# Operands of the second token group written straight into the hop tiles, operand pairs stored together, and the first steps of the layer put in another order

## The chip, the cores and the metric

One core of one Trainium2 chip runs the whole kernel. The metric is device time in microseconds of one launch, the median of several runs. TensorE (PE) multiplies, VectorE (DVE) and ScalarE (ACT) work on tiles, GpSimd (POOL) casts and copies now and then, and SyncE (SP) issues nearly all DMAs. Each engine takes its instructions in the order in which they stand in its own row; semaphores hold it until its inputs are there.

## The reference

One layer with 2048 tokens and 256 context tokens of width 1024; both head groups read one input projection, and one output projection joins them.

```python
shift, scale, gate = split(silu(c) @ w_ada + b_ada, 3)          # ada; also for c_ctx
h  = rmsnorm(x, norm_w)   * (1 + scale)   + shift               # (2048, 1024)
hc = rmsnorm(ctx, norm_w) * (1 + scale_c) + shift_c             # (256, 1024)
p  = h  @ w_in                                                  # 5*1024 + 4*1024 columns
pc = hc @ w_in[:, :5*1024]
q, v, f_f, f_b ... = hgrn_prep(p)                               # 8 heads of 128
o_f, o_b = chunk_scan(forward), chunk_scan(backward)            # states begin from the context's
y_hg = rmsnorm(o_f + o_b, onorm_w) * silu(p[gate columns])
y_cv = bg * conv3(cg * h_conv, conv_w) * silu(gate_conv)
out  = rmsnorm(x + gate * (concat(y_hg, y_cv) @ w_out), final_norm_w)
```

## The kernel before

**Products.** The 2048 tokens are four groups of 512 (`GW`), x0 to x3. A product of a group with a pair of weight column blocks is made in seven products over half the tokens instead of eight (`seven`), in fp16 with a high and a low part: three matmuls per step, L890, L891, L892. The weights give seven operands (A11, S1, ...), and each group gives seven: B11, T1, T2, B21, T3, B22, T4 (`OPS`). One operand of a group is 128 x 2 (high, low) x 4 (`HK`) x 256 (`HW`) in fp16, 512 KB. Group x0 is special in its first use, where its plain high and low parts (four tiles `plain`) are multiplied without the seven (`plain` units).

**Windows.** The work is a list of windows; a window is one head (or one block of the convolution) on one group. Windows 0 to 3 are head 0 on groups 0 to 3; windows 4 to 7 head 1, and so on. In each, the products of a few units (q, v, f, the gate) run on PE, while the chunk scan of the head (Q, K, A, S on DVE, ACT and PE) runs between them. The context's products (`ctx` units, with the operands `hc`) run in the windows of head 0.

**Operands of a group.** For groups 1 to 3 `norm_group` makes the operands: it loads four row tiles of 128 tokens (`load`, tiles xt), sums their squares on ACT (`square`, L238), scales them by the reciprocal root (`norm`, L244 on ACT and L246 on DVE, in turn), and then makes four turns. A turn (`turn`, `combine`, L321 on) transposes two feature blocks on PE (L253, eight transposes), applies scale and shift on ACT (L274), makes sums on DVE (L328, L329, L331, L337), casts high parts on ACT or POOL (L279, L281) and subtracts to get low parts on DVE (L298), into `pair` tiles, and stores each operand's share in DRAM (`Hd`, L300): seven stores in a turn. When all four turns of a group are stored, `prefetch` loads the seven operands into tiles of `hp` (L1306, `hop`), one DMA of 128 rows of 4 KB each, as far as the nine (`HOPS`) hop tiles allow; `freed` and `taken` count them, and `set_ready` lets a group's loads begin. Every later window that uses the group loads the seven operands again. For x0, whose plain parts are in SBUF, B11, B21 and B22 are stored by `store_first` and the T operands come from four `late` turns (`late_turn`) that read the raw values back from DRAM (`Xd`).

**Order.** What one engine does in which order is set in the program: the products of a window call `tick`, and steps (`paced`, with weights in `PACE`) are issued between them, spread by `merge_steps` over the window. In before, window 0 holds the context's norm and turns, x1's norm and four turns, and x2's loads, norm and first turn; window 1 holds x2's other turns and x3's loads, norm and first turn; window 2 x3's other three; window 3 x0's four late turns. A step is issued behind a given instruction with `tc.issue_after` (`behind` does it for weights, behind the last product that is kept).

**Start.** `modulate` multiplies the conditioning with w_ada as its tiles arrive (1 MB per block of 128 features) and transposes x0's raw blocks (`raw`) between; `modulate_end` takes the result out of PSUM (`ada_r`, L209), transposes it (`ada_t`, L212); `affine` turns it into scale and shift (`ab`).

Of the kernel before, what the change touches and what calls it, by code (L numbers as in the profile page):

```python
# [60 lines left out]
def hybrid_layer(ctx: ExitStack, tc, x, cx, w_ada, b_ada, w_in, w_out, fnorm_w, small_d, masks, ident_d, sel_d, out):  # L61
# [19 lines left out]
    Hd = [{o: dp.tile([P, 2, HK, HW], F16, name=f"Hd{g}{o}", tag=f"Hd{g}{o}") for o in OPS} for g in range(NG)]  # L81
# [125 lines left out]
    def modulate_end(pada):  # L207
        ada_r = ring("ada_r")
        V.tensor_copy(ada_r, pada)  # L209
        ptr = pa_t("ada_t")  # L210
        for q in range(4):
            PE.transpose(ptr[:, q * P:(q + 1) * P], ada_r[:, q * P:(q + 1) * P], ident)  # L212
        V.tensor_tensor(ada, ptr.rearrange("p (q j m) -> p j q m", q=4, j=4)[:, :, :, 0:2],
                        sub(bada, 0, [[4, 4], [1, 4], [0, 2]]), ALU.add)

# [10 lines left out]
    def norm_group(ntile, src, row0, m, nm, first_ops=None, space=q_tile):  # L226
        n = ntile * P
        xs = []
        ssq = sp.tile([P, 16], F32, tag="ssq", name=f"ssq_{nm}", bufs=4)

# [6 lines left out]
        def square(i):  # L237
            S.activation(junk, xs[i], AF.Square, accum_out=ssq[:, i:i + 1])  # L238

        def norm():  # L240
            rstd = rsqrt(ssq[:, :ntile], ntile, 1.0 / D, nm)
# [8 lines left out]
        def transposed(k):  # L250
            pt = pa_t(f"xT_{nm}{k}")
# [72 lines left out]
        def combine(k, a, b, whole):  # L324
# [10 lines left out]
            else:  # L335
# [8 lines left out]
                [paced(0.0, lambda k=k: raw(k)) for k in range(KT)])  # L344
# [12 lines left out]
    def behind(fn):  # L357

        if not last_keep:
            return fn()  # L360
        with tc.issue_after(last_keep[-1].ins):
            fn()
# [661 lines left out]
    def wo_at(name, hl, k):  # L1024
        return wo_home(name, hl)[:, k // HK, k % HK, :]
# [287 lines left out]
    extra_a21 = [[a21_[:, hl, :, i * P:(i + 1) * P] for hl in range(2)] for i in range(2)]  # L1313
    taken[0] = len(plain) + 1 + NCH
# [11 lines left out]
    pada = modulate(lambda k: first[4][k][1](), lambda: next_w(0))  # L1326
# [3 lines left out]
    modulate_end(pada)  # L1330
# [3 lines left out]
    affine(1, 7)  # L1334
    x_norm = [None, x1_norm] + [norm_group(NCH, x, g * GW, 0, f"x{g}") for g in range(2, NG)]

    def store_first():
        for o in ("B11", "B21", "B22"):
            r, half = int(o[1]) - 1, int(o[2]) - 1
            for i in range(HK // 2):  # L1340
                for hl in range(2):
                    SY.dma_start(Hd[0][o][:, hl, 2 * i:2 * i + 2],
                                 plain[r * HK // 2 + i][:, hl, :, half * HW:(half + 1) * HW])

    def set_ready(g):
        ready[0] = max(ready[0], g)
        if g == 1:
# [19 lines left out]
    def run(wi, units, steps):  # L1367
# [20 lines left out]
        for un, (wk, kind, i, fn) in enumerate(units):  # L1388
# [22 lines left out]
            elif kind == "plain":  # L1411
                ps = bank(turn_bank[0], f"u{ui}")
                turn_bank[0] = 1 - turn_bank[0]
                for half in range(2):
                    hs = slice(half * HW, (half + 1) * HW)
                    for k in range(KT):
                        op, kk = w.ops[f"A{i}{k // HK + 1}"], k % HK
                        r = [plain[k // 2][:, hl, k % 2, hs] for hl in range(2)]
# [6 lines left out]
            elif kind == "pair":  # L1425
# [5 lines left out]
                seven(w.ops.get, lambda o, hl, k, i=i: C[i][o][:, hl, k, :], HK, GW, f"{ui}", pair_step,  # L1431
# [167 lines left out]
```

## Time and profile before

| | |
|---|---|
| median of 3 runs | 2181.78 us (2180.26 to 2185.07) |
| profiled execution | 2187.49 us, span 2185.7 |
| granted TensorE clock, mean | 0.990 |
| PE busy | 2089.4 us |
| DVE busy | 1652.1 us |
| ACT busy | 1169.2 us |
| start of the plain products | 44.69 us |
| first product on x1's, x2's, x3's operands | 97.06, 155.77, 197.09 us |

The times of the rows below are counted from the start of the span of the profiled execution. In the timeline a row is a run of equal instructions on one engine: start, time to the end of the last of them, engine, line, operation, output and inputs; in brackets the time that the engine stood idle before it and who released it. An engine that stands idle does no harm unless it is the one that sets the end.

### The profile page before, as it was taken

What the parts mean: (1) busy time and instruction counts of PE and PEld (TensorE: products, weight loads), DVE (VectorE), ACT (ScalarE), POOL (GpSimd) and SP (SyncE); (2) the same over time, 40 slices, a digit from 0 to 9 for tenths busy, and PEclk for the clock granted to TensorE, in tenths of its full rate; (3) what the DMA queues carried; (4) which work ended last, traced back from release to release, by engine and by line L of the source; (5) the groups of instructions that cost most, each with busy time, mean ns of one, the idle gap of its engine ahead of it and who ended that gap; (6) DMA issues with size and microseconds to landing.
All of it is one profiled execution on the core that took longest, in us unless ns stands there. A gap on an engine that the chain in (4) does not pass through costs nothing.

```text
span 2185.7 us, 51899 instructions
## 1 busy us (share of the span) xinstructions
PE 2089.4 (96%) x21563; PEld 1468.2 (67%) x21563; DVE 1652.1 (76%) x3456; ACT 1169.2 (53%) x2341; POOL 157.9 (7%) x239
## 2 busy tenths in 40 slices
PE   5789999999999999999999999999999999999998
PEld 2677688888887988888889887444444444444443
DVE  7887777878779778788687786677787656687775
ACT  7865556666557565666675654344444423333332
POOL 0211111010010110101111000000000000000000
PEclk9999999999999999999999999999999999999999
DMA  9766533433243333333633448923443205633321
GB/s 349 238 205 208 181 132 103 141 116 105 86 159 107 114 114 125 111 108 128 194 123 123 140 156 260 274 97 121 135 139 98 66 30 181 213 124 108 127 85 58
DMA packets 196464, 310.41 MB, mean 142 GB/s; under 512 B 13570, under 2 KB 126594, under 8 KB 194436
## 3 DMA queue, kind: packets, MB, share of 16 engines
q1 hardware_dynamic: 194068, 303.16, 42.5%
q8 instruction: 169, 2.77, 0.5%
q10 hardware_dynamic: 2160, 3.93, 0.5%
q14 instruction: 67, 0.55, 0.1%
HBM read 241.77 MB, written 65.27 MB: 140 GB/s over the span
## 4 chain that ended last, share of the span: by engine, by line
PE 66%; DVE 18%; ACT 8%; DMA 5%; issue 2%; POOL 1%; SPq 0%; POOLq 0%; ACTq 0%; DVEq 0%
PE sa L890 8%; PE sa L891 8%; PE sa L892 8%; PE sb L890 4%; PE sb L891 4%; PE sb L892 4%; PE sa_o L890 2%; PE sa_o L891 2%; PE sa_o L892 2%; DVE e_p L152 2%; PE A L599 2%; PE sc L890 2%; PE sc L892 2%; PE sc L891 2%; DVE K L453 2%
## 5 line engine op out<-in xcount | busy, mean ns | idle before, releaser
L453 DVE TENSOR_TENSOR K<-K,tot 128x512 f32<-128x512 f32 x192 | 133.6, 696 | 60.1 <-PE A L627 27.6
L891 PEld LDWEIGHTS <-e_p 128*128 128x128 f16 x1368 | 134.1, 98 | 60.4 <-issue 10.9
L890 PEld LDWEIGHTS <-e_p 128*128 128x128 f16 x1368 | 134.1, 98 | 59.9 <-DMA hop1T<-Hd1T 2.6
L892 PEld LDWEIGHTS <-e_p 128*128 128x128 f16 x1368 | 134.2, 98 | 52.8 <-issue 1.8
L460 DVE TENSOR_TENSOR Q<-Q,tot 128x512 f32<-128x512 f32 x192 | 132.4, 690 | 44.3 <-PE A L599 30.9
L569 ACT ACTIVATE km<-K 128x512 f32<-128x512 f32 x160 | 109.0, 686 | 69.5 <-DVE K L453 60.0
L890 PEld LDWEIGHTS <-whib_p 128*128 128x128 f16 x912 | 89.3, 98 | 41.2 <-issue 5.0
L890 PEld LDWEIGHTS <-whia_p 128*128 128x128 f16 x912 | 89.4, 98 | 38.5 <-DMA hop3B<-Hd3B 2.8
L891 PEld LDWEIGHTS <-whib_p 128*128 128x128 f16 x912 | 89.4, 98 | 38.2 <-issue 4.1
L891 PEld LDWEIGHTS <-whia_p 128*128 128x128 f16 x912 | 89.3, 98 | 37.7 <-issue 5.6
L892 PEld LDWEIGHTS <-wlob_p 128*128 128x128 f16 x912 | 89.4, 98 | 34.7 <-issue 0.5
L892 PEld LDWEIGHTS <-wloa_p 128*128 128x128 f16 x912 | 89.4, 98 | 34.4
L151 ACT ACTIVATE e_p<-ws_p,sc_p 128x512 f16<-128x512 f32 x108 | 77.2, 717 | 53.4 <-DVE ws_p L413 33.3
L576 POOL COPY qm<-Q 128x512 f32<-128x512 f32 x64 | 55.7, 870 | 630.2 <-DVE Q L460 627.2
L635 POOL COPY A<-Ac 32x128 f32<-32x128 f32 x128 | 68.3, 534 | 371.2 <-ACT A L631 367.2
L897 ACT ACTIVATE u<-sa,sx_w 128x256 f32<-128x256 f32 (+1 forms) x114 | 59.8, 525 | 59.2 <-PE sa L892 48.7
L897 ACT ACTIVATE p<-sb,sx_w 128x256 f32<-128x256 f32 (+1 forms) x114 | 59.4, 521 | 52.9 <-PE sb L892 52.3
L897 ACT ACTIVATE p<-sa,sx_w 128x256 f32<-128x256 f32 (+1 forms) x114 | 59.1, 518 | 47.4 <-PE sa L892 46.6
L152 DVE SCALAR_TENSOR_TENSOR e_p<-ws_p,sc_p,e_p 128x512 f16<-128x512 f32 x108 | 78.5, 742 | 1.0 <-ACT e_p L151 1.0
L813 ACT ACTIVATE cv<-c,small 128x512 f32<-128x512 f32 (+1 forms) x36 | 24.2, 674 | 97.6 <-DVE c L831 52.9
L378 ACT ACTIVATE junk<-ws_p 128x1024 f16<-128x1024 f32 x72 | 75.7, 1051 | 0.2
L151 ACT ACTIVATE hiS_o<-y_o,sc_y 128x1024 f16<-128x1024 f32 x32 | 36.8, 1149 | 72.6 <-PE sa_o L891 32.2
(865 smaller groups left out, 6972.1 us busy)
## 6 DMA issues: line engine op xcount, KB each, us to landing
ws_p<-in_w_in SPq DMA_DIRECT2D x72, 512.0 KB, 4.4
y_o<-yT SPq DMA_DIRECT2D x32, 512.0 KB, 4.2
xt_x<-in_x SPq DMA_DIRECT2D x16, 512.0 KB, 4.6
wa<-in_w_ada SPq DMA_DIRECT2D x16, 512.0 KB, 10.2
Gd<-zs SPq DMA_DIRECT2D x32, 256.0 KB, 3.2
wos<-in_w_out SPq DMA_DIRECT2D x32, 256.0 KB, 3.9
sg<-Gd SPq DMA_DIRECT2D x32, 256.0 KB, 3.8
yT<-y SPq DMA_DIRECT2D x32, 256.0 KB, 2.2
```

What stands on the lines that cost most here:

```text
L151: S.activation(hi, src, AF.Copy, scale=st[:, 0:1])
L152: V.scalar_tensor_tensor(lo, src, st[:, 0:1], hi, ALU.mult, ALU.subtract)
L378: S.activation(junk.rearrange("p (k n) -> p k n", k=KT), stage[i], AF.Abs, accum_out=r)
L453: V.tensor_tensor(m, m, sub(cur, nb + 1, [[2, np_], [-(nb + 1), 2], [0, B]]), ALU.mult)
L460: V.tensor_tensor(m, m, sub(cur, 1, [[2, np_], [nb - 1, 2], [0, B]]), ALU.mult)
L569: S.activation(sub(s.km, 0, [[2 * B, n // (2 * B)], [B, 2], [1, B]]), mix(s.K, n, B, n // (2 * B)), AF.Copy)
L576: G.tensor_copy(sub(qm, 0, [[2 * B, n // (2 * B)], [B, 2], [1, B]]), mix(s.qf, n, B, n // (2 * B)))
L635: G.tensor_copy(A3[js, :, js], s.Ac[js])
L890: PE.matmul(ps, hi[:, k], rh, start=start and k == 0, stop=False, skip_group_check=not start)
L891: PE.matmul(ps, hi[:, k], right(name, 1, k), start=False, stop=False, skip_group_check=not start)
L892: PE.matmul(ps, lo[:, k], rh, start=False, stop=k == nk - 1, skip_group_check=not start)
L897: last_keep.append(S.activation(r, ps, AF.Copy, scale=sx))
```

## The change

Seven things change together.

1. The layout of an operand in SBUF is [128, 4, 2, 256] (block, part, token) rather than [128, 2, 4, 256]. In DRAM the operands lie in rows that belong to a pair: B11 and T3, T1 and T2, B21 and B22 side by side (`Hr`), T4 alone. A turn stores a pair with one DMA, four stores in a turn; a load of one operand of a pair collects 1024 pieces of 512 bytes.
2. In the start, the last two raw transposes of x0 are issued behind the transposes of ada, `ada_r` is copied half by DVE and half by ACT, the context's `affine` is issued behind x0's third low part, and the squares and scales of a group are issued behind the casts and lows of the group before (`follow`).
3. x1's operands are written straight into the tiles that window 1 reads (`own1`: four hop tiles and three Q tiles), with casts of 256 columns; they are stored to DRAM in window 1 (`store_own`, seven DMAs). x1's row tiles lie in weight staging tiles.
4. x2's loads, norm and first turn move from window 0 to window 1, x3's norm stays late in window 1's list and its first turn moves to window 2. x2's row tiles lie in hop tiles, x3's in Q tiles that `own1` frees.
5. x0's four late turns move from window 3 to windows 4 and 5, two each.
6. The weights of the gate are loaded in window 0 still, behind x1's last transposes.
7. The counts in `freed` and `taken` are adapted.

The diff's core:

```diff
+    ROWS = (("B11", "T3"), ("T1", "T2"), ("B21", "B22"), ("T4",))
+    Hr = [{r: dp.tile([P, HK, 2, len(r), HW], F16, name=f"Hd{g}{r[0]}", tag=f"Hd{g}{r[0]}") for r in ROWS}
+          for g in range(NG)]
+    Hd = [{o: Hr[g][r][:, :, :, i] for r in ROWS for i, o in enumerate(r)} for g in range(NG)]
...
-        V.tensor_copy(ada_r, pada)
+        V.tensor_copy(ada_r[:, :HW], pada[:, :HW])
+        S.activation(ada_r[:, HW:], pada[:, HW:], AF.Copy)
...
         def square(i):
-            S.activation(junk, xs[i], AF.Square, accum_out=ssq[:, i:i + 1])
+            follow(casts.get(before), lambda: S.activation(junk, xs[i], AF.Square, accum_out=ssq[:, i:i + 1]))
 
         def norm():
+            follow(lows.get(before), scaled)
...
+            if direct:
+                for i, op in enumerate(ops):
+                    cast(eng, direct[op][:, k, 0], row[:, i * HW:(i + 1) * HW])
+                    low.append(V.tensor_tensor(direct[op][:, k, 1], row[:, i * HW:(i + 1) * HW], direct[op][:, k, 0],
+                                               ALU.subtract))
+                return
...
-            V.tensor_tensor(lo, row, hi, ALU.subtract)
-            for i, op in enumerate(ops):
-                SY.dma_start(Hd[row0 // GW][op][:, :, k], pair[:, :, i])
+            low.append(V.tensor_tensor(lo, row, hi, ALU.subtract))
+            g = row0 // GW
+            if n2 == 2:
+                SY.dma_start(Hr[g][ops][:, k], pair)
+            else:
+                SY.dma_start(Hd[g][ops[0]][:, k], pair[:, :, 0])
...
-    x1_norm = norm_group(NCH, x, GW, 0, "x1", None, wa_hop)
+    own1 = {}
+    x1_norm = norm_group(NCH, x, GW, 0, "x1", None, stage_tile, own1)
...
+    turned = modulate_end(pada)
+    for k in (KT - 2, KT - 1):
+        follow(turned, first[4][k])
...
+    for n_, o in enumerate(OPS):
+        own1[o] = hop_tile(f"hop1{o}") if n_ < 4 else qp.tile([P, HK, 2, HW], F16, tag="Q", name=f"hop1{o}", bufs=6)
+    hop[1] = own1
...
-            early = (ctx_norm[1] + ctx_norm[2] + n1[1] + n1[2] if wi == 0 else n1[2][1:]) + ready_
+            early = (ctx_norm[1] + ctx_norm[2] + n1[1] if wi == 0 else []) + n1[2] + ready_
             if wi == 0:
                 more_params()
-                for _, st in n2[0]:
+                early.insert(0, paced(0.1, store_first))
+                early += [paced(0.1, lambda: next_w(1, 6))]
+            if wi == 1:
+                store_own()
+                for _, st in n1[0]:
                     st()
-                early += [paced(0.1, store_first)]
...
-                early += n2[1] + n2[2][:1]
+                taken[0] += NCH
+                early = n1[1] + [paced(14.0, lambda: None)] + early
+            if n2 is not None and wi:
+                early += [paced("pause", lambda: None)] + n2[0] + n2[1]
             extra = early + extra
-        elif wi == NG - 1:
-            extra = first[3] + extra
+        elif wi in (NG, NG + 1):
+            extra = first[3][(wi - NG) * 2:(wi - NG) * 2 + 2] + extra
```

On PE, at the end of window 0 before: x2's first transposes (xT, two feature blocks x20 and x24 and one of the next turn) stand between the context's last product (u) and window 1's first product (sa on hop1B11).

```order
L1407 MATMUL u6_1123<-hc_128,wloa_p8_277 128x256
L253 MATMUL xT_x20_1082<-ident_132,xt_x20_488 128x128
L253 MATMUL xT_x24_1089<-ident_132,xt_x20_488 128x128
...
L253 MATMUL xT_x24_1089<-ident_132,xt_x23_494 128x128
L253 MATMUL xT_x21_1181<-ident_132,xt_x21_490 128x128
L890 LDWEIGHTS whia_p24_219
L890 MATMUL sa_7_1164<-hop1B11_1013,whia_p24_219 128x256
```

The same place now:

```order
L1444 LDWEIGHTS wloa_p8_265
L1444 MATMUL u6_1008<-hc_116,wloa_p8_265 128x256
L917 LDWEIGHTS whia_p24_207
L917 MATMUL sa_7_1060<-hop1B11_474,whia_p24_207 128x256
L918 LDWEIGHTS whia_p24_207
L918 MATMUL sa_7_1060<-hop1B11_474,whia_p24_207 128x256
```

No transposes stand there any more; x2's first are now 824 rows into PE's list, in window 1. On SP, before, the loads of x1's operands (hop1) stand among the stores of x1's and x2's turns (Hd1, Hd2; 256 pieces):

```order
L1306 DMA hop1B11_1013<-Hd1B11_94 128x2048
L300 DMA Hd1T4_100<-hpT4_x13_979 256x1x256
L1306 DMA hop1T1_1015<-Hd1T1_95 128x2048
L1306 DMA hop1T2_1017<-Hd1T2_96 128x2048
L1306 DMA hop1B21_1019<-Hd1B21_97 128x2048
L300 DMA Hd2T1_102<-hpT1_x20_1099 256x1x256
L300 DMA Hd2T2_103<-hpT1_x20_1099 256x1x256
```

There are no hop1 loads for window 1 now. At the next such place, the loads of x2's operands (hop2) ahead of window 2, SP has now, with x3's row tiles (xt_x30 to xt_x33) among them:

```order
L252 DMA xt_x30_1810<-in_x 128x1024
L252 DMA xt_x31_1812<-in_x 128x1024
L328 DMA Hd2T1_96<-hpT1_x23_1665 128x1024
L328 DMA Hd2B11_95<-hpB11_x23_1670 128x1024
L328 DMA Hd2B21_97<-hpB21_x23_1674 128x1024
L330 DMA Hd2T4_98<-hpT4_x23_1679 128x512
L252 DMA xt_x32_1814<-in_x 128x1024
L1333 DMA hop2B11_1787<-Hd2B11_95 128x8x256
L1333 DMA hop2T1_1789<-Hd2T1_96 128x8x256
...
L1333 DMA hop2T4_1799<-Hd2T4_98 128x2048
L252 DMA xt_x33_1816<-in_x 128x1024
```

A turn's stores are four rather than seven, a load of a pair's operand is 128 x 8 pieces of 256 elements, and x3's fourth row tile is loaded behind all hop2 loads. On PE, window 2's products run from row 1203 to 1743 of the list; x3's first transposes now stand there, among the products on hop2 and the scan's matrices (A0):

```order
L917 MATMUL sc_11_2286<-hop2B21_1793,whia_p8_264 128x256
L274 MATMUL xT_x30_1914<-ident_120,xt_x30_1810 128x128
L274 MATMUL xT_x34_1921<-ident_120,xt_x30_1810 128x128
L626 MATMUL A0_0_1_1967<-q_0_1_1283,ks_0_1_1686 32x32 x9
L274 MATMUL xT_x30_1914<-ident_120,xt_x31_1812 128x128
```

They are rows 1450 on; the last transposes of x3 end at row 1554. Before, x3's first turn stood in window 1 (row 1163) and its last in window 2 (rows 1576 to 1583).

## Rows read from the trace of the kernel before

**Rows 1.** The page: busy us (share of span) and instructions by engine.

```profile
PE 2089.4 (96%) x21563; PEld 1468.2 (67%) x21563; DVE 1652.1 (76%) x3456; ACT 1169.2 (53%) x2341; POOL 157.9 (7%) x239
```

**Rows 2.** Windows: stretch, us, busy by engine, granted clock, DMA share, GB/s.

```profile
50.00:100.00 50.00, 39.58 (x322) 34.02 (x321) 41.45 (x114) 42.80 (x76) 11.25 (x17) 0.88 0.77 244
100.00:150.00 50.00, 42.14 (x562) 34.45 (x560) 44.85 (x111) 33.82 (x62) 8.56 (x13) 0.91 0.72 239
150.00:200.00 50.00, 45.57 (x584) 40.58 (x582) 38.52 (x80) 26.76 (x51) 10.14 (x15) 0.99 0.48 150
200.00:250.00 50.00, 43.94 (x543) 30.49 (x542) 41.28 (x90) 29.16 (x55) 7.58 (x10) 1.00 0.78 252
250.00:300.00 50.00, 49.89 (x709) 43.70 (x708) 35.89 (x89) 27.46 (x66) 3.87 (x6) 1.00 0.38 122
```

**Rows 3.** Windows of 10 us, columns as in group 2.

```profile
90.00:100.00 10.00, 5.35 (x26) 4.56 (x27) 7.65 (x19) 6.48 (x11) 1.58 (x2) 0.52 0.81 272
40.00:50.00 10.00, 5.04 (x24) 3.07 (x25) 8.98 (x29) 7.82 (x15) 3.64 (x4) 0.58 0.93 349
...
230.00:240.00 10.00, 9.02 (x71) 6.80 (x71) 10.00 (x18) 6.27 (x13) 2.69 (x4) 1.00 0.82 250
```

**Rows 4.** Timeline of PE at the starts of units and windows.

```profile
44.69 0.37 PE L1419 MATMUL u<-hop,whia_p 128*128 128x256 f16 x1 [2.59 <-ACT hop L281]
...
94.35 2.42 PE L253 MATMUL xT_x<-ident,xt_x 128*128 128x128 f32 x10 [7.07 <-DVE xt_x L246]
...
97.06 0.37 PE L890 MATMUL sa<-hop1B,whia_p 128*128 128x256 f16 x1 [0.30 <-DMA hop1B<-Hd1B]
...
108.72 0.28 PE L890 MATMUL sa<-hop1T,e_p 128*128 128x256 f16 x1 [2.48 <-DMA hop1T<-Hd1T]
...
155.77 0.27 PE L890 MATMUL sa<-hop2B,whia_p 128*128 128x256 f16 x1
...
197.09 0.28 PE L890 MATMUL sa<-hop3B,whia_p 128*128 128x256 f16 x1 [2.49 <-DMA hop3B<-Hd3B]
...
220.43 0.18 PE L139 MATMUL ss_p<-rb_p 128*128 128x1 bf16 x1 [2.48 <-DVE rb_p L382]
```

**Rows 5.** Timeline around the conditioning's transposes.

```profile
39.35 0.68 DVE L209 COPY ada_r<-pada 128x512 f32<-128x512 f32 x1
...
40.17 0.30 PE L212 MATMUL ada_t<-ident,ada_r 128*128 128x128 f32 x1 [1.47 <-ACT junk L238]
```

**Rows 6.** DVE groups, 69 to 94 us: busy us, mean ns, idle before.

```profile
L298 DVE TENSOR_TENSOR hpB_x<-h_x,hpB_x 128x512 f16<-128x512 f32 x8 | 5.4, 687 | 1.4 <-POOL hpB_x L279 1.3
...
L298 DVE TENSOR_TENSOR hpT_x<-h_x,hpT_x 128x256 f16<-128x256 f32 x4 | 1.7, 419 | 0.5 <-POOL hpT_x L279 0.5
```

**Rows 7.** Timeline: scales of x1 and x2, last lows of x2 and x3.

```profile
65.34 1.18 ACT L244 ACTIVATE xt_x<-xt_x,rsy_x 128x1024 f32<-128x1024 f32 x1
...
93.54 1.42 DVE L246 TENSOR_SCALAR xt_x<-xt_x,rsy_x 128x1024 f32<-128x1024 f32 x2
...
132.66 0.43 DVE L298 TENSOR_TENSOR hpT_x<-h_x,hpT_x 128x256 f16<-128x256 f32 x1 [0.30 <-POOL hpT_x L279]
...
190.49 0.42 DVE L298 TENSOR_TENSOR hpT_x<-h_x,hpT_x 128x256 f16<-128x256 f32 x1 [0.19 <-POOL hpT_x L279]
```

**Rows 8.** Timeline of SP: issues of loads of operands.

```profile
192.47 0.56 SPq L1306 DMA_DIRECT2D hop3B<-Hd3B  x1
...
453.55 0.32 SPq L1306 DMA_DIRECT2D hop10T<-Hd2T  x1
...
1332.14 1.69 SPq L951 DMA_DIRECT2D C0B<-Hd0B  x1
```

**Rows 9.** Windows: two stretches full of loads, columns as in group 2.

```profile
10.00:30.00 20.00, 12.90 (x64) 4.43 (x66) 16.22 (x40) 13.77 (x22) 0.00 (x0) 1.00 1.03 410
1330.00:1340.00 10.00, 10.00 (x94) 9.00 (x92) 6.40 (x14) 2.74 (x6) 0.00 (x0) 1.00 1.18 299
```

**Rows 10.** Tile hop10B on PE: durations ns min/median/max, first and last start.

```profile
L890 PE MATMUL sa<-hop10B,whia_p x8: 272/273/273, 468.2 to 481.9; 128*128 128x256 f16 x8
```

More of the change, by code (lines that the diff above doesn't have):

```diff
@@ L224, in affine, with follow, norm_group @@
         V.tensor_scalar(ab[:, m], ab[:, m], hsc[m][:, 0:1], None, ALU.mult)
-    def norm_group(ntile, src, row0, m, nm, first_ops=None, space=q_tile):
+    def follow(marks, fn):
+        if not marks:
+            return fn()
+        with tc.issue_after(marks[-1].ins):
+            fn()
+    lows, casts = {}, {}
+    def norm_group(ntile, src, row0, m, nm, first_ops=None, space=q_tile, direct=None):
         n = ntile * P
@@ L229, in norm_group @@
         ssq = sp.tile([P, 16], F32, tag="ssq", name=f"ssq_{nm}", bufs=4)
+        before = None if first_ops is not None else "x0" if m else f"x{row0 // GW - 1}"
+        low, high = lows.setdefault(nm, []), casts.setdefault(nm, [])
         def load(i):
@@ L254, in transposed, with raw @@
             return pt
-        def raw(k):
-            pt = transposed(k)
+        def raw(k, space=pa_t):
+            pt = transposed(k, space)
             raws[k] = ring(f"h32_{nm}{k}")
-            if k % 2:
+            if k % 2 and space is pa_t:
                 V.tensor_copy(raws[k], pt)
@@ L343, in norm_group @@
                 [paced("late", lambda k=k: late_turn(k)) for k in range(HK)],
-                [paced(0.0, lambda k=k: raw(k)) for k in range(KT)])
+                [lambda k=k: raw(k, pa_t if k < KT - 2 else px_t) for k in range(KT)])
     class W:
@@ L357, in behind @@
     def behind(fn):
[L359 to L362, printed above, removed]
+        follow(last_keep, fn)
     def load_pair(col0, col1, nm, own=False, a21_at=None):
@@ L1298, in hybrid_layer @@
     for wi, g in enumerate(group_of):
-        if g is not None and wi and g != group_of[wi - 1]:
+        if g is not None and wi > 1 and g != group_of[wi - 1]:
             queue += [(wi, g, o) for o in OPS]
@@ L1324, in hybrid_layer @@
     next_w(0)
-    pada = modulate(lambda k: first[4][k][1](), lambda: next_w(0))
+    pada = modulate(lambda k: first[4][k]() if k < KT - 2 else None, lambda: next_w(0))
     ctx_norm = norm_group(2, cx, 0, 1, "c")
@@ L1333, in hybrid_layer, with store_own @@
         st()
-    affine(1, 7)
-    x_norm = [None, x1_norm] + [norm_group(NCH, x, g * GW, 0, f"x{g}") for g in range(2, NG)]
+    follow(lows["x0"][:3], lambda: affine(1, 7))
+    x_norm = [None, x1_norm] + [norm_group(NCH, x, g * GW, 0, f"x{g}", None, wa_hop if g == 2 else q_tile)
+                                for g in range(2, NG)]
+    for n_, o in enumerate(OPS):
+        own1[o] = hop_tile(f"hop1{o}") if n_ < 4 else qp.tile([P, HK, 2, HW], F16, tag="Q", name=f"hop1{o}", bufs=6)
+    hop[1] = own1
+    def store_own():
+        for o in OPS:
+            SY.dma_start(Hd[1][o], own1[o])
     def store_first():
@@ L1340, in store_first @@
             for i in range(HK // 2):
-                for hl in range(2):
-                    SY.dma_start(Hd[0][o][:, hl, 2 * i:2 * i + 2],
-                                 plain[r * HK // 2 + i][:, hl, :, half * HW:(half + 1) * HW])
+                SY.dma_start(Hd[0][o][:, 2 * i:2 * i + 2],
+                             plain[r * HK // 2 + i][:, :, :, half * HW:(half + 1) * HW])
     def set_ready(g):
         ready[0] = max(ready[0], g)
-        if g == 1:
+        if g == 2:
             freed[0] += NCH
@@ L1417, in run @@
                         op, kk = w.ops[f"A{i}{k // HK + 1}"], k % HK
-                        r = [plain[k // 2][:, hl, k % 2, hs] for hl in range(2)]
+                        r = [plain[k // 2][:, k % 2, hl, hs] for hl in range(2)]
                         PE.matmul(ps[:, hs], op[0][:, kk], r[0], start=k == 0, stop=False)
@@ L1445, in run @@
             pace[1] += 1
-        if wi == 0 and units[-1][1] == "ctx" and len(units) > 2:
+        if wi == 0:
             freed[0] += 5
```

41 lines of the change are left out of this document (18 added, 23 removed).

## The prediction

> **What bounds the kernel now.** I read the page first, then the windows view, then PE's timeline, then SP's. PE is busy for 2089.4 us, 96% of the span [rows 1]; the matmuls are the same before and after, so the time can only move by what PE waits for, or by its clock. The windows view says where it waits: between 50 and 250 us PE is busy 39.58, 42.14, 45.57 and 43.94 of 50 us, and from 250 on 49.89 [rows 2]. So what the change can win or lose at its beginning is won or lost before 250, and a microsecond there is one at the end, since PE is full behind it. The idle time of those four slices is 200 - 171.2 = 28.8 us. The second loss is the clock: 0.58 in 40 to 50 and 0.52 in 90 to 100 [rows 3], each time behind a wait; for those two stretches TensorE ran mostly at 1.2 GHz.
>
> The timeline shows the waits one by one [rows 4]: 2.59 us before the plain products (44.69), 7.07 before x2's first transposes (94.35), 0.30 before the first product of window 1 (97.06), 2.48 for a load of x1's operands (108.72), 2.49 for x3's operands (197.09, the start of window 3), and 2.48 (220.43). Window 2 starts at 155.77. The second column to look at is DVE: 41.45, 44.85, 38.52 and 41.28 of 50 us in the same slices [rows 2]. DVE has 34 us of slack against PE's 29. It is the engine that prepares the operands of groups 1 to 3 (turns and their casts), and the change removes no turn. That is why I don't believe that all of PE's waits can go.
>
> **The head.** The last two raw transposes go behind those of ada, and ada_r is copied half by DVE and half by ACT. Now DVE's copy of the whole tile starts only at 39.35, behind a raw copy of the same size (0.69), takes 0.68, and PE waits 1.47 us until 40.17 [rows 5]. With the raw copy out of the way and two halves side by side on two engines, ada_r is there 0.69 + 0.68/2 = 1.0 us sooner from these rows alone, and up to 1.7 with the square's place on ACT, which the row at 40.17 names as what ended the wait [rows 5]. The context's squares now stand behind x0's casts, which takes some 0.6 us more from the ACT work ahead of the first cast. I put the plain products at 42.4, so -2.3 us (bounds -0.5 and -3.0, the latter a little over the whole 2.59 wait).
>
> **Window 0.** x1's operands are written directly into the hop tiles; no store, no load. x2's norm and first turn leave window 0: PE's 7.07 us wait at 94.35 goes, with the half clock that follows, and so do the 0.30 and the 2.48 of the loads. What then ends last is DVE on x1. One turn is three 128x512 lows at 0.69 us and, on 128x256, one low and four sums of about 0.42 [rows 6], 4.2 us busy, some 4.4 with what lies between; four turns 17.6. With the larger lows cut in 256-wide pieces a turn has 11 operations of 0.42 (they overlap by some 0.08), about 3.8 us, four 15; with the first head's Q and K steps (about 3.5) 18.5. x1's last scale ends at 65.34 + 1.18 = 66.5 on ACT [rows 7], transposes and h_x take two or three more, so the last low stands at 86 to 88 if DVE has nothing else. The first product needs only the first tile's last low and starts at about 85.5: 11.6 us ahead of 97.06 (bounds 84.5 and 88).
>
> **Window 1.** It took 58.7 us (97.06 to 155.77). It now also holds x2's norm and first turn, DVE 1.42 for two scales [rows 7] plus the chain of small operations of the norm (an estimate: a dozen at 0.16 to 0.3, 2.4) and a turn of 4.4, that is 8 us on DVE, beside the 44.85 of 50 it had [rows 2]. So the window is DVE's: x2's last low lies at 131 to 135, about where it was (132.66 + 0.42 [rows 7]), though PE is 11 us ahead. The wait that the change removes in front of window 1 returns inside it, in part. Behind the last low come the stores of one turn and the seven loads. These loads are the other half of the change: a pair is stored with one DMA, but a load then collects pieces of 512 bytes. An old load issues in 0.32 us [rows 8]. The nearest rows for small pieces are the C loads of the convolution, 1.69 us each back to back [rows 8], with 299 GB/s against 410 in the load stretch at 10 to 30 us [rows 9]. The price of a load between those ends is 1.75 us (512 KB at 299 GB/s) against 1.28; a product takes 1.31. While PE eats them as they land, each of six loads costs 0.44 us, 2.6 us a set. That is the upper bound; with a lead it is nothing. Window 2 starts at 140.3 by that (134 + 4.6 for a load, as in front of window 3 [rows 4, 8], + 1.7 for the feed), -15.5 us; bounds 138.5 and 143.
>
> The Trainium skill, page "DMA: Bandwidth & Descriptors", section "Specifications", gives 512 B as the least transfer for line rate. By it these loads would cost what the old ones did, and the 2.6 us here and the 3.5 below would be nothing: rival (d). The 299 against 410 GB/s [rows 9] does not agree with it, so I go by the rows.
>
> **Window 2.** It took 41.3 us. Before, x3's norm and first turn were done in window 1, and its other three turns here; now all four turns are here. Two of x3's four row tiles are loaded before x2's last stores, the third before and the fourth behind the seven hop2 loads on SP, all waiting for Q tiles that x1's operands hold until window 1's last products (T3, B22 and T4). What is queued behind a waiting SP there is the hop2 loads themselves. The transposes of x3 stand 46% down PE's row of window 2 (row 1450 between 1203 and 1743): 19 us in. From there DVE has four turns (4.4 each, 17.8) and the head's Q and K levels (some 8 us of this stretch): 26 us. x3's last low is therefore at 140.3 + 18.5 + 26, about 185, where it was 190.9 (190.49 + 0.42 [rows 7]). The first load was issued at 192.47 [rows 8] and the product stood at 197.09 [rows 4], 4.6 us after. With 512-byte pieces 6 rather than 4.6: window 3 starts at about 191, -6 us; PE, which has 41 us of work there, waits some 8 to 10 us at the end of window 2 instead. So of the 15.5 us gained, 9.5 are given back here. Bounds: -20, if DVE does the turns as they come and PE never waits, and +1, if they start 6 us later and the load is slow.
>
> **Window 3 and after.** The four late turns of x0 (four DVE-heavy steps, DVE 10.00 of 10 us in 230 to 240 [rows 3], with PE waiting 2.48 at 220.43 [rows 4]) move to windows 4 and 5, where DVE has 14 of 50 us free (35.89 in 250 to 300 [rows 2]) and PE has no wait. -3.5 us in window 3 (bounds -1 and -5, the latter near all of its 6 us of idle), +1 in windows 4 and 5 (0 and +3). In the other windows a hop load is issued well ahead: a T load of set 10 at 453.55 [rows 8], the first product on that set's B operands at 468.2 [rows 10], 14.7 us later. DMA's share there is 0.38 [rows 2]. So the 0.44 us per load are hidden; what hides them is a lead of some 10 us. Where that cover is gone, in front of the C loads, DMA stands at 1.18 [rows 9], and 14 hop loads of sets 34 and 35 lie among them: 6 x 0.45 per set, and two partly hidden sets, +3.5 us (0 and +6).
>
> **Sum, against the profiled execution** (2187.49 us, span 2185.7 and 1.8 around it): -6 at window 3's start, -3.5, +1, +3.5 = -5.0, so 2182.5 profiled. The median of the runs shown is 5.7 us less than the profiled run, so 2181.8 - 5.0 = 2176.8 us.
>
> **Rivals.** (a) The whole gain stays. DVE's 34 us of slack [rows 2] suffice, x3's turns spread over window 2 as they are issued, and window 3 starts near 180: -17, with -3.5 and +1, and the C loads' price small (+1): -18, or 2163. For it: DVE was never above 44.85 of 50 in these windows; against it: x3's first turn stands 46% into window 2, and four turns are 18 us. (b) The gain is given back entirely, with the small pieces landing late everywhere that the queue is full: window 3 at 194 (-3), -2, +1, +4: 0, or 2181.8. (c) Slower, by one mechanism: x3 is late. If its fourth row tile waits, behind the hop2 loads, for the last Q tile, and the norm with it, the first turn stands at window 2's start + 26 rather than + 18.5; the last low is then at 192.5 and window 3 starts at 198.5 to 200, +2.5. PE has then waited some 16 us, and behind a wait of 7 us the clock stood at 0.52 for a slice [rows 3], which costs up to 4 us more of window 3. With -2, +1 and +4 the sum is +9, 2191. It decides from a first turn later than about 24 us into window 2. (d) The small pieces cost nothing: the C loads were slow because fourteen and more of them were queued at once, and a lone set of seven lands like the old ones, 4.6 us after its issue. Then window 2 starts 1.7 to 2.6 us sooner, window 3 with it, and the +3.5 falls away: -5 - 2.6 - 3.5 = -11, 2170.7. For it: the old loads, too, land late where the queue is full; against it: 299 GB/s at a DMA share of 1.18 [rows 9], which is engine time, not waiting.
>
> For the clock: in 40 to 50 and 90 to 100 it was low directly behind waits of 2.59 and 7.07 us. The Trainium skill, page "TensorE: Matmul & The Clock Gate", section "What's actually happening", describes the slow clock as the state that an idle array falls back to; by it a wait of 8 to 10 us at the end of window 2 would cost window 3's first products double time, which is rival (c)'s last term and is not in the -5.0.
>
> **How the numbers follow.** Forecast -5 (its own range -10 to -1) 0.38; (a) 0.22; (b) 0.10; (c) 0.20; (d) 0.10. A measurement of this kernel can tell 0.2% (4.4 us) from no change. Of the forecast 0.22 lies below 2177.4 and 0.16 above; (a) and (d) are faster, (b) is 0.08 same and 0.02 slower, (c) slower. Together faster 0.54, same 0.24, slower 0.22. The range reaches from (a)'s own lower bound, -22 (window 3's bounds -17 and -5, nothing behind it), to (c)'s +9: 2160 to 2191.
>
> **What would show it.** Right: the first plain product near 42.4; the first product on hop1 near 85.5, on hop2 near 140, on hop3 near 191, with the wait in front of that last one 6 us or more and named by DMA or DVE; DVE above 9 of 10 in 140 to 185; no wait in 300 to 1300 us. Wrong: a hop3 start before 185, when DVE was not the bound (rival a); a first x3 turn later than 24 us into window 2 (c); a wait for hop loads in the steady windows, which would make the small pieces a price of every window; PE's busy share unchanged in 200 to 250, when the late turns were not what it waited for.

## The result, and the profile after

The changed kernel takes 2191.89 us, the kernel before 2185.09 us (medians of 14 runs each); the ratio is 1.0034 with a 95% interval of 1.0025 to 1.0043. It is 7 us slower. (The profiled execution after, 2196.23 us, is the slowest of its 14, so the two traces lie 8.7 us apart, the medians 6.8.) The prediction said 2176.8, 5 us below the median known then, with a range to 2191: wrong in sign, and just outside the range.

The page of the profiled execution after, to be read against [rows 1]: PE's busy time is nearly the same, the span 8.7 us longer (2185.7 before).

```profile
span 2194.4 us, 51787 instructions
...
PE 2094.0 (95%) x21563; PEld 1469.2 (67%) x21563; DVE 1654.4 (75%) x3467; ACT 1170.6 (53%) x2351; POOL 159.9 (7%) x243
```

The windows of 50 us (columns as in [rows 2]) say where:

```profile
50.00:100.00 50.00, 43.73 (x375) 37.73 (x374) 41.74 (x137) 39.78 (x80) 10.35 (x20) 0.96 0.54 174
100.00:150.00 50.00, 38.82 (x526) 31.50 (x526) 44.63 (x91) 34.85 (x66) 10.38 (x14) 1.00 0.60 190
150.00:200.00 50.00, 39.18 (x504) 31.96 (x505) 36.44 (x79) 26.95 (x46) 8.00 (x14) 0.86 0.48 147
200.00:250.00 50.00, 48.27 (x599) 35.69 (x598) 34.29 (x75) 29.38 (x52) 7.55 (x6) 1.00 0.66 195
```

PE gains 4.2 us in 50 to 100 and 4.3 in 200 to 250, and loses 3.3 in 100 to 150 and 6.4 in 150 to 200, where the mean granted clock is 0.86. So the beginning won most of what it was to win, and window 2 lost more. PE's timeline has the starts (the rows that answer to [rows 4]):

```profile
42.50 0.27 PE L1456 MATMUL u<-hop,whia_p 128*128 128x256 f16 x1 [2.13 <-ACT hop L302]
...
88.02 0.27 PE L917 MATMUL sa<-hop1B,whia_p 128*128 128x256 f16 x1 [3.52 <-ACT f_c L523]
...
145.42 0.27 PE L917 MATMUL sa<-hop2B,whia_p 128*128 128x256 f16 x1 [0.99 <-DMA hop2B<-Hd2B]
...
204.75 0.27 PE L917 MATMUL sa<-hop3B,whia_p 128*128 128x256 f16 x1 [1.58 <-DMA hop3B<-Hd3B]
```

The first products on hop5, hop6, hop35 and C0 (the convolution's first operands) come from the view of those tiles. A table makes the ledger plain; the last column is how far the changed kernel is behind (+) or ahead (-) there.

| first product | before | after | predicted | after - before |
|---|---|---|---|---|
| plain | 44.7 | 42.5 | 42.4 | -2.2 |
| window 1 (hop1) | 97.1 | 88.0 | 85.5 | -9.0 |
| window 2 (hop2) | 155.8 | 145.4 | 140.3 | -10.4 |
| window 3 (hop3) | 197.1 | 204.8 | 191 | +7.7 |
| window 5 (hop5) | 286.9 | 288.4 | | +1.5 |
| window 6 (hop6) | 319.8 | 323.1 | | +3.3 |
| hop35 | 1339.7 | 1345.4 | | +5.7 |
| C0 | 1363.9 | 1376.2 | | +12.3 |
| span's end | 2185.7 | 2194.4 | | +8.7 |

So the time is lost in three places: window 2, 2.5 us between hop30 and hop31 (left open below), and 6.6 us between hop35 and C0. Behind that 3.6 us come back: the trace of before has a wait of 2.4 us for ACT just before 1870 us, and a clock of 0.91 in 1860 to 1880, that the changed kernel has not.

Window 2 takes 59.3 us instead of 41.3. In it DVE first stands idle and is then full (windows of 10 us, columns as before):

```profile
150.00:160.00 10.00, 8.52 (x73) 6.98 (x74) 1.45 (x3) 2.96 (x6) 0.00 (x0) 1.00 0.86 248
160.00:170.00 10.00, 8.73 (x178) 6.83 (x179) 6.11 (x19) 9.06 (x15) 1.29 (x2) 1.00 0.03 7
170.00:180.00 10.00, 5.01 (x104) 3.63 (x93) 9.39 (x20) 6.12 (x10) 2.28 (x4) 0.85 0.45 154
180.00:190.00 10.00, 6.91 (x100) 5.41 (x97) 9.69 (x21) 3.09 (x5) 2.57 (x6) 0.50 0.47 132
```

DVE is busy for 1.45 of 10 us in 150 to 160 and for 9.4 and 9.7 in 170 to 190; PE then has 5.0 and 6.9 of 10 us and a clock of 0.85 and 0.50, and that without one long wait. Its waits in window 2, grouped (total, times, longest):

```profile
PE A L654 <- DVE Q L487: 1.8, 1, 1.8
PE A L626 <- POOL qm L603: 1.8, 1, 1.8
PE sb L917 <- DMA hop2T<-Hd2T: 1.6, 1, 1.6
PE xT_x L274 <- ACT h_x L295: 1.4, 1, 1.4
PE A L644 <- DVE Q L487: 1.3, 1, 1.3
```

The longest is 1.8 us: a chain of short waits for DVE, POOL and ACT. What DVE waited for between 147.5 and 161 stands in three timelines, of SP, ACT and DVE:

```profile
139.80 0.58 SPq L1333 DMA_DIRECT2D hop2B<-Hd2B  x1
...
149.97 1.94 SPq L1333 DMA_DIRECT2D hop2T<-Hd2T  x1
152.01 0.38 SPq L252 DMA_DIRECT2D xt_x<-in_x  x1
```

```profile
159.83 1.06 ACT L256 ACTIVATE junk<-xt_x 128x1024 f16<-128x1024 f32 x1 [0.97 <-DMA xt_x<-in_x]
```

```profile
153.60 0.48 DVE L928 SCALAR_TENSOR_TENSOR f<-sc,sx_w,p 128x256 f32<-128x256 f32 x1 [6.11 <-PE sc L919]
...
161.01 0.17 DVE L131 TENSOR_SCALAR rsv_x<-ssq_x 128x4 f32<-128x4 f32 x1 [3.66 <-ACT junk L256]
...
167.69 0.40 DVE L358 TENSOR_TENSOR ht_x<-h_x 128x256 f32<-128x256 f32 x1
...
197.65 0.41 DVE L325 TENSOR_TENSOR hpT_x<-h_x,hpT_x 128x256 f16<-128x256 f32 x1
```

The seven loads of x2's operands hold SP from 139.80 to 151.9, x3's last row tile is issued behind them, its square is summed at 159.83, the norm begins at 161.01, x3's first turn at 167.69, and its last low ends at 198.06. But this tile ends only the last 3.7 us of DVE's idle time. Before that it waits 6.11 us, and then twice a little over 1 us, for the first products of window 2 itself, whose results f it takes out of PSUM: nothing of x3 stands ahead of them in DVE's row. After the last low come the loads for window 3.

The second loss lies where the convolution's operands are loaded. PE's waits for operands between 1325 and 1400 us:

```profile
PE sb L917 <- DMA hop35T<-Hd3T: 3.2, 1, 3.2
...
PE sb L917 <- DMA hop35B<-Hd3B: 1.5, 1, 1.5
```

Before they were 0.7 and 0.2 us:

```profile
PE sa L890 <- DMA hop35T<-Hd3T: 0.7, 1, 0.7
```

The clock is 0.83 in 1350 to 1370, behind these waits, where before it was 1.00 and 0.97. In the steady windows from hop6 to hop30 the difference stays at 3.1 to 3.3 us: the small pieces cost nothing there.

### The profile page after: what moved, and what is told of

Read it like the earlier page. It is cut to its first block, busy times and chain, and to the rows that moved or that the text cites. A ratio compares the mean times of both kernels' runs of the same rounds, so it can differ in the third digit from the quotient of the medians.

```text
span 2194.4 us, 51787 instructions
## 1 busy us (share of the span) xinstructions
PE 2094.0 (95%) x21563; PEld 1469.2 (67%) x21563; DVE 1654.4 (75%) x3467; ACT 1170.6 (53%) x2351; POOL 159.9 (7%) x243
## 4 chain that ended last, share of the span: by engine, by line
PE 65%; DVE 19%; ACT 6%; DMA 4%; issue 3%; POOL 1%; SPq 0%; POOLq 0%; ACTq 0%; DVEq 0%
PE sa L917 8%; PE sa L919 8%; PE sa L918 8%; PE sb L917 4%; PE sb L918 4%; PE sb L919 4%; PE sa_o L917 2%; PE sa_o L919 2%; PE sa_o L918 2%; DVE e_p L158 2%; PE sc L917 2%; PE sc L919 2%; PE sc L918 2%; PE A L626 2%; DVE K L480 2%
## 5 line engine op out<-in xcount | busy, mean ns | idle before, releaser
L487 DVE TENSOR_TENSOR Q<-Q,tot 128x512 f32<-128x512 f32 x192 | 133.0, 693 | 44.7 <-PE A L626 30.6
L917 PEld LDWEIGHTS <-whib_p 128*128 128x128 f16 x912 | 89.8, 98 | 45.9 <-issue 5.0
L918 PEld LDWEIGHTS <-whia_p 128*128 128x128 f16 x912 | 89.7, 98 | 45.0 <-issue 12.3
L918 PEld LDWEIGHTS <-whib_p 128*128 128x128 f16 x912 | 89.9, 99 | 42.4 <-issue 7.7
L919 PEld LDWEIGHTS <-wlob_p 128*128 128x128 f16 x912 | 89.8, 98 | 35.1 <-issue 0.6
L919 PEld LDWEIGHTS <-wloa_p 128*128 128x128 f16 x912 | 89.8, 98 | 34.6
L924 ACT ACTIVATE p<-sb,sx_w 128x256 f32<-128x256 f32 (+1 forms) x114 | 59.3, 520 | 56.4 <-PE sb L919 55.7
```

What stands on the lines that cost most here:

```text
L487: V.tensor_tensor(m, m, sub(cur, 1, [[2, np_], [nb - 1, 2], [0, B]]), ALU.mult)
L917: PE.matmul(ps, hi[:, k], rh, start=start and k == 0, stop=False, skip_group_check=not start)
L918: PE.matmul(ps, hi[:, k], right(name, 1, k), start=False, stop=False, skip_group_check=not start)
L919: PE.matmul(ps, lo[:, k], rh, start=False, stop=k == nk - 1, skip_group_check=not start)
L924: last_keep.append(S.activation(r, ps, AF.Copy, scale=sx))
```

## The experiments

The kernel before, run again beside each set of experiments, took 2184.2 and 2184.4 us; every ratio is to that. Two theories stood first. Theory A: the 512-byte pieces are the cause, since the hop2 loads push x3's last tile back. Theory B: the order is, whatever a load costs.

**The pieces undone.** In DRAM each operand lies by itself, loads are rows of 4 KB; the order stays:

```diff
+    APART = (0, 1, 2, 3)
+    for g in APART:
+        Hd[g] = {o: dp.tile([P, HK, 2, HW], F16, name=f"Ha{g}{o}", tag=f"Ha{g}{o}") for o in OPS}
...
-            if n2 == 2:
+            if g in APART:
+                for i, op in enumerate(ops):
+                    SY.dma_start(Hd[g][op][:, k], pair[:, :, i])
+            elif n2 == 2:
```

> The changed kernel with one part undone: in DRAM each operand lies by itself again, so that a load is 128 rows of 4 KB (and a turn stores seven times); the order of the steps stays the changed one. Theory A (the small pieces): the seven loads of x2's operands took 12.2 us on SP (139.80 to 151.9) and x3's last row tile, issued behind them at 152.01, landed near 159.8; with loads of about 0.5 us it comes 8 us sooner, the norm with it, DVE's empty stretch at 150 to 160 shrinks, and window 3 starts at about 195 rather than 204.8. The wait for hop35 (3.2 + 1.5 us) goes too. Sum -14 to -16 on 2191.9: about 2177, ratio to before 0.996. Theory B (the order): x3's four turns lie behind tiles that come free only at the end of window 1, whatever a load costs; window 3 starts at 202 or later, and only the hop35 waits and what follows them go: about 2186, ratio 1.000 to 1.001.

Measured: 2184.72 us, ratio to before 1.0001 (0.9991 to 1.0010), about 7 us better than the changed kernel. Window 3 starts at 202.8, not 195. The loads do take 3.5 us now, but the norm does not come sooner by as much; ACT and DVE in that kernel:

```profile
155.43 0.63 ACT L539 ACTIVATE f<-f 128x512 f32<-128x512 f32 x1 [1.11 <-DVE f L934]
...
156.81 1.04 ACT L259 ACTIVATE junk<-xt_x 128x1024 f16<-128x1024 f32 x1
...
158.37 1.04 ACT L259 ACTIVATE junk<-xt_x 128x1024 f16<-128x1024 f32 x1
```

```profile
152.07 0.48 DVE L934 SCALAR_TENSOR_TENSOR f<-sc,sx_w,p 128x256 f32<-128x256 f32 x1 [3.14 <-PE sc L925]
...
159.54 0.17 DVE L134 TENSOR_SCALAR rsv_x<-ssq_x 128x4 f32<-128x4 f32 x1 [4.14 <-ACT junk L259]
```

The squares no longer wait for a DMA. They stand in ACT's row behind the activations of f (L539), which wait for DVE, which waits for window 2's own products; the norm begins at 159.54 rather than 161.01. So in window 2 theory A is worth 2 us and theory B the rest. At hop35 theory A holds: no wait for DMA is left there.

**x3's tiles early.** The pieces stay at 512 bytes; x3's four row tiles are loaded in window 1 ahead of the loads of x2's operands, two of them in hop tiles (SP issues three of them by 76.7 us and the fourth at 122.64, where it was 152.01):

```diff
+    def x3_tile(nm):
+        return (q_tile if nm[-1] in "01" else wa_hop)(nm)
...
-                taken[0] += NCH
-                early = n1[1] + [paced(14.0, lambda: None)] + early
+                taken[0] += NCH + 2
+                early = n1[1] + [paced(14.0, lambda: None)] + n1[2][:3] + n2[0] + n1[2][3:] + ready_
             if n2 is not None and wi:
-                early += [paced("pause", lambda: None)] + n2[0] + n2[1]
+                early += [paced("pause", lambda: None)] + n2[1]
```

> The changed kernel with x3's four row tiles loaded at the start of window 1, two of them in hop tiles instead of Q tiles, so that none stands behind the loads of x2's operands; the loads keep their 512-byte pieces. The scheduler then puts x3's first transposes 13% into window 2 rather than 46%. Theory A: the small pieces still hold hop2 (about 12 us for seven) and hop3, and the hop35 waits stay; the lateness of x3's norm goes: window 3 starts at 192 to 196, -9 to -13, about 2181, ratio 0.998. Theory B: the late tile is all there is to it; window 3 starts near 188 to 190, -15 to -17, about 2176, ratio 0.996. If window 3 still starts later than 202, neither holds and the four turns themselves (DVE) are too much for one window.

Measured: 2179.95 us, ratio 0.9979 (0.9969 to 0.9988): 12 us better than the changed kernel, and faster than before. The tile view and the windows (10 us):

```profile
L917 PE MATMUL sa<-hop3B,whia_p x20: 272/273/421, 191.0 to 260.2; 128*128 128x256 f16 x20
```

```profile
150.00:160.00 10.00, 9.41 (x193) 7.80 (x193) 7.40 (x15) 6.80 (x12) 2.27 (x3) 1.00 0.76 243
...
170.00:180.00 10.00, 9.36 (x112) 8.18 (x101) 9.58 (x18) 5.14 (x9) 3.87 (x6) 1.00 0.52 154
180.00:190.00 10.00, 9.00 (x82) 8.19 (x80) 9.76 (x24) 4.77 (x10) 1.34 (x2) 1.00 0.68 238
```

Window 3 starts at 191.0, 13.8 us sooner. DVE does 7.40 of 10 us where it did 1.45, PE has 9.4 and 9.0 where it had 5.0 and 6.9, and the clock stays at 1.00, 2.4 GHz. DVE now begins x3's norm at 142.00, ahead of window 2's products, and its first turn at 153.15:

```profile
142.00 0.17 DVE L131 TENSOR_SCALAR rsv_x<-ssq_x 128x4 f32<-128x4 f32 x1
...
153.15 0.42 DVE L358 TENSOR_TENSOR ht_x<-h_x 128x256 f32<-128x256 f32 x1
```

That shows the cause in window 2, the place of x3's norm and turns behind the late tile. The place moved in the rows of PE, ACT and DVE at once; that it is DVE's empty stretch that cost the time is read from the two traces. The time lies near theory A's (2181), not B's (2176). The wait for hop35 stays, as theory A has it there:

```profile
PE sb L917 <- DMA hop35T<-Hd3T: 4.4, 1, 4.4
```

**Both repairs.** The two edits together.

> Both repairs at once: 4 KB rows and x3's tiles loaded early. Theory A: the repairs overlap in window 2 (the fourth tile is late in only one way), so it is 3 to 6 us better than the kernel with 4 KB rows alone: about 2172, ratio 0.994. Theory B: about the same as early tiles plus the hop35 waits: 2170 to 2172. Window 3 should start at 183 to 188, at least 9 us ahead of the kernel before.

Measured: 2174.14 us, ratio 0.9953 (0.9936 to 0.9970), the fastest of all, 10 us faster than before. Window 3 starts at 191.4, not at 183 to 188 as expected, so 4 KB rows add nothing in window 2 once the tiles are early. They add 6 us in all; in the traces 4.7 of it lie between hop35 and C0 (25.3 us instead of 30.0), where that wait has shrunk (Ha is the DRAM tile of an operand that lies by itself). Another 3.1 us lie between hop30 and hop31, where the kernels differ without a known cause (see below). The wait for hop35 is now:

```profile
PE sa L923 <- DMA hop35T<-Ha3T: 0.7, 1, 0.7
```

**The pieces alone on the kernel before.** Pairs stored with one DMA, 512-byte loads, nothing else of the change:

```diff
-            for i, op in enumerate(ops):
-                SY.dma_start(Hd[row0 // GW][op][:, :, k], pair[:, :, i])
+            g = row0 // GW
+            if n2 == 2:
+                SY.dma_start(Hr[g][ops][:, k], pair)
+            else:
+                SY.dma_start(Hd[g][ops[0]][:, k], pair[:, :, 0])
```

> The kernel before with only the layout of the change: pairs stored with one DMA, loads of 512-byte pieces; the order of steps stays the one before. Theory A: each set of seven loads in front of a window costs some microseconds there (hop1, hop2, hop3), and hop35 waits as in the changed kernel: +7 to +12 us, ratio 1.003 to 1.006. Theory B: the stores that it saves pay for the early loads, and only the hop35 waits show: 0 to +6, ratio 1.000 to 1.003.

Measured: 2195.64 us, ratio 1.0048 (1.0033 to 1.0063), theory A's size but not all its places. Windows 1 to 3 start no later than before (95.8, 155.4, 197.0); the loss is in window 3 (2.7 us up to hop5, with a clock of 0.89 to 0.94 in four slices of 10 us where it was 1.00) and between hop35 and C0 (5.9 us). PE's waits in 185 to 290 and in 1325 to 1400:

```profile
PE gate_r L1053 <- DMA wg<-in_w_ada: 3.4, 3, 2.5
PE sa L896 <- DMA hop3B<-Hd3B: 2.7, 1, 2.7
```

```profile
PE sb L896 <- DMA hop35T<-Hd3T: 4.0, 1, 4.0
...
PE sb L896 <- DMA hop35B<-Hd3B: 1.2, 1, 1.2
```

**Whose pieces.** x3's tiles early, and 4 KB rows for group x3 alone (`APART = (3,)`).

> x3's tiles early, and 4 KB rows for group x3 alone, so that the loads of hop3 and hop35 are large while those of x2 (hop2, hop34) keep their 512-byte pieces. Theory C (the set's own pieces): the 4.4 us wait for hop35 goes as in the kernel with 4 KB rows for all, about 2175. Theory D (the queue): hop34's five small loads, which stand ahead of the convolution's loads on SP, lengthen the queue by about 5 x 1.2 us whoever comes after; the wait for hop35 stays at 2 to 4 us, about 2178.

Measured: 2175.94 us, ratio 0.9967 (0.9955 to 0.9978). Most of the 6 us comes back with x3's set alone, 4 of them; a wait of 1.8 + 0.7 us is left at hop35. Theory C has most of it, and the queue (D) a rest:

```profile
PE sb L923 <- DMA hop35T<-Ha3T: 1.8, 1, 1.8
PE sa L923 <- DMA hop35T<-Ha3T: 0.7, 1, 0.7
```

**The late turns alone on the kernel before.**

```diff
-        elif wi == NG - 1:
-            extra = first[3] + extra
+        elif wi in (NG, NG + 1):
+            extra = first[3][(wi - NG) * 2:(wi - NG) * 2 + 2] + extra
```

> The kernel before with x0's four late turns moved from window 3 to windows 4 and 5, two each, and nothing else. By the prediction window 3 loses its 2.48 us wait for rb_p and part of the rest, -3.5 us (bounds -1 and -5), and windows 4 and 5 give back 1: -2.5 in all, ratio 0.9989. The traces of the two kernels say more for the two windows behind window 3 (89.8 us between the first products on hop3 and hop5 before, 83.6 in the changed kernel) and less behind (32.9 and 34.7): -4.4, ratio 0.998. Rival: what the changed kernel saved there was not the late turns but the hop3 loads and the DMA queue, then 0 to -1.

Measured: 2179.10 us, ratio 0.9976 (0.9966 to 0.9985): -5 us. From the first product on hop3 to that on hop5 84.7 us instead of 89.8, from there to hop6 34.2 instead of 32.9:

```profile
L890 PE MATMUL sa<-hop3B,whia_p x20: 272/273/421, 195.3 to 263.8; 128*128 128x256 f16 x20
L890 PE MATMUL sa<-hop5B,whia_p x8: 272/272/273, 280.0 to 292.2; 128*128 128x256 f16 x8
```

That is -3.8 in the windows that the edit touches; the other 1.8 us that this trace is ahead stand already at window 3's start. The rival, that the queue and not the turns gave it, falls.

**The late turns back, in the kernel with both repairs.** The same edit the other way.

> The fastest kernel so far (4 KB rows, x3's tiles early) with the late turns back in window 3. If they cost what the changed kernel shows, windows 3 and 4 are 5 to 6 us longer and window 5 1 to 2 shorter: +4, 2178, ratio 0.997. If in that kernel window 3 has room for them now, +0 to +1: 2174 to 2175.

Measured: 2179.62 us, ratio 0.9977 (0.9966 to 0.9987): +5 against 2174.14. Moving them is worth the same there.

**The start alone on the kernel before.**

```diff
-        V.tensor_copy(ada_r, pada)
+        V.tensor_copy(ada_r[:, :HW], pada[:, :HW])
+        S.activation(ada_r[:, HW:], pada[:, HW:], AF.Copy)
...
-    modulate_end(pada)
+    turned = modulate_end(pada)
+    for k in (KT - 2, KT - 1):
+        with tc.issue_after(turned[-1].ins):
+            first[4][k]()
```

> The kernel before with only the start of the change: ada_r copied half by DVE and half by ACT, the last two raw transposes behind those of ada. The plain products start near 42.5 rather than 44.69, as in the changed kernel. Theory: window 0 is bound by DVE on x1's chain and x2's norm, whose own inputs come by DMA and don't move; then of 2.2 us at most 1 reaches the first product on hop1, ratio 0.9995 to 1.0. Rival: everything in windows 0 to 3 hangs on the head, and the whole -2.2 us arrives: ratio 0.999.

Measured: 2184.05 us, ratio 1.0001 (0.9992 to 1.0011): no gain is seen. The plain products start at 43.5, 1.2 us sooner rather than 2.2, and the interval, some 2 us to either side, can't tell whether so small a gain arrives. The tile view says what became of it:

```profile
L891 PE MATMUL sa<-hop3B,whia_p x20: 272/273/283, 192.6 to 270.2; 128*128 128x256 f16 x20
L891 PE MATMUL sa<-hop5B,whia_p x8: 272/272/273, 286.2 to 300.5; 128*128 128x256 f16 x8
```

Window 3 starts at 192.6, 4.5 us ahead of before, more than the head itself gave; window 5 at 286.2, 0.7 ahead. From hop3 to hop5 it took 93.6 us instead of 89.8 and gave the gain back. PE's waits there, and the two slices of 10 us in which its clock was below 1.00:

```profile
PE ss_p L139 <- DVE rb_p L383: 3.1, 1, 3.1
PE sa L891 <- DVE tot L467: 1.6, 1, 1.6
PE A L600 <- issue: 1.6, 1, 1.6
```

```profile
210.00:220.00 10.00, 6.91 (x113) 3.74 (x100) 7.60 (x22) 6.53 (x13) 1.35 (x3) 0.86 0.66 180
220.00:230.00 10.00, 9.58 (x64) 4.82 (x62) 9.15 (x20) 3.69 (x7) 1.75 (x2) 0.80 0.90 255
```

The first two waits are for DVE, on the weights' sizes and the scan, between the late turns (the one for rb_p was 2.48 before [rows 4]), and the clock adds to them.

## Why the prediction was wrong, by its own steps

**The head** was right: 42.50 against 42.4 predicted.

**Window 0 and window 1: the mechanisms right, the sizes off.** The wait of 7.07 us went, and DVE bounded x1 as said, but more than said: its last low ended at 92.7, not at 86 to 88, and window 1 started at 88.0, not 85.5. PE's wait for the evacuation of the context's f, which stood at 2.50 before, is 3.52 and now directly in front of window 1; ACT does that evacuation behind x1's casts, which wait for DVE. Window 1 was DVE's, 9.0 to 9.7 of 10 us busy from 90 to 140; x2's last low ended at 138.9 rather than 134. The load and its feed were 6.5 us against 6.3. Window 2 therefore started 5.1 us later than predicted: 4.9 by DVE's work in windows 0 and 1, which I had put at too little, and 0.2 by the load.

**Window 2: the term that failed.** The prediction had x3's last low at window 2's start + 18.5 + 26, that is 185, and window 3 at 191. The trace has 198.1 and 204.8, 14 later. By the terms: 5.1 from window 2's start; 3.8 because the transposes began where I put them (18.8 us in) but the first sums on DVE only at 22.3; 4.4 because the four turns and the levels took 30.4 us instead of 26; 0.7 from the load. Of these 30.4 us the turns are 15.8, less than the 17.8 predicted, DVE's other steps 13.1 rather than "some 8", and some 1.5 idle. So the mis-sized term is DVE's other work: by these rows, what it could not do while it stood idle, waiting for window 2's products, stands between the turns. The prediction's own sign, DVE above 9 of 10 from 140 to 185, failed: it was 6.5, 1.5 and 6.1 in 140 to 170. I had seen x3's fourth tile behind the hop2 loads and counted it as a place in PE's row; I had not asked what DVE does meanwhile. From 147.5 to 161.0 it has nothing to do for 12 us, and that work is missing at the end. The prediction's "PE waits 8 to 10 us" was right in sum (8.8 from 164 to 200); but it came as many short waits, and with them the clock fell to 0.50, as it had fallen to 0.52 in the kernel before behind the long one [rows 3]. That price stood only in rival (c).

**Rival (c), x3 late,** is what happened, at 9 us predicted and 7 to 9 measured. That the size fits is in part luck: it had window 3 at 198.5 to 200 (204.8 measured), 4 us of slow clock in window 3 (the clock fell before it) and -2 + 1 for the late turns (-4.4). Its condition was put wrong: it was to decide from a first turn later than 24 us into window 2, and 22.3 was enough, as DVE has more other work there than reckoned. Its reason was the tile behind the loads; the first experiment shows that the loads' duration was a small part (2 us), and the second that the place in the order was the larger (13.8, of which 2.0 stand already at window 2's start).

**Window 3 and after.** The late turns were put at -3.5 + 1 = -2.5; measured -5.2 alone on the kernel before (-3.8 by its trace), 5.5 when they were put back, and -4.4 in the changed kernel by its trace. The mechanism was right, the size some half of it. The small pieces in the steady windows: hidden, as predicted. At hop35 +3.5 was predicted; the waits are 4.7 us against 0.9, 3.8 more, the way from hop35 to C0 is 6.6 us longer, slow clock included, and undoing the pieces gives back 6 to 7 of the whole time. The Trainium skill's rule behind rival (d) (page "DMA: Bandwidth & Descriptors", section "Specifications", 512 B for line rate) does not hold in the full queue of this kernel: the layout alone, its loads in pieces of 512 bytes and its paired stores, made the kernel before 1.0048 times as long, and in 1340 to 1350 the DMA engines of the changed kernel moved 294 GB/s at a share of 1.20, those of the kernel with the pieces undone 390 at 1.07.

**"A microsecond before 250 is one at the end"** was too simple. It was read from PE being full behind 250 [rows 2], and from hop7 to hop30 it holds: all ten kernels take 851 to 852 us for that stretch. But a gain in front of window 3 may stay in window 3: the head alone was 4.5 us ahead there and 0.7 two windows later. It need not: with both repairs and the late turns in window 3 the start at 192.1 is 5.0 us ahead of before, and 4.5 of it are left at hop5 (282.4). So the late turns as such don't eat it; why window 3 took longer with the head alone, beyond the waits shown, is not settled.

Two more things stay open. Between the first products on hop30 and hop31 the changed kernel takes 31.5 us and the one before 29.0; a wait for POOL is 1.7 us instead of 0.8 there and the clock of one slice 0.83, but the kernels with 4 KB rows show both lengths (31.4 and 28.5), so the pieces don't explain it, and the changed order by itself doesn't. And the wait of 2.4 us for ACT just before 1870 us in the kernel before is absent in the changed one; nothing in the change touches it, and three of the other kernels have it too, at 0.9 to 1.8 us.

## What to carry to other kernels

When an engine that is not the bound has little slack over a stretch (here DVE, 34 of 200 us), a step's place counts twice: what it delays, and the idle time that it leaves on that engine ahead of it, which cannot be had back. So after a move, read the row of the engine that does the moved work for its empty slices, not only the row of the engine that waits for the result. And price a layout where its transfers meet a full queue, not where they have a lead: the small pieces were free from window 7 to window 30 and cost 6 to 11 us in all in the few places where the next product stood behind the load.

## What was not expected of the hardware

TensorE's granted clock fell to 0.50, 1.2 GHz, for a whole slice (180 to 190) without any wait over 1.8 us; PE was busy 5.0 and 6.9 of 10 us in 170 to 190. The matmuls show the two levels (timeline of PE in the changed kernel, start and time of one):

```profile
189.94 0.42 PE L919 MATMUL sa<-hop2B,wloa_p 128*128 128x256 f16 x1
...
191.69 0.27 PE L917 MATMUL sb<-hop2T,whib_p 128*128 128x256 f16 x1
```

In the kernel with x3's tiles early, with 9.4 and 9.0 of 10, it stayed at 1.00. And loads in pieces of 512 bytes, one behind another, hold SP as well as the DMA engines: seven of them took 12.1 us of its time in front of window 2, seven of 4 KB rows 3.5, and a load of something else behind them waits for both. One by itself in a steady window, near 490 us, held SP for 0.52 us.
